# Second moving tile from the bank, rotation of the keys two steps sooner, angle steps spread over later steps

## The chip, the cores and the metric

The kernel runs on one core of a Trainium2 chip. Five engines work side by side, each through its own instructions in order: TensorE (PE, with its weight loads PEld), VectorE (DVE), ScalarE (ACT), GpSimd (POOL) and SyncE (SP), which here only issues DMAs. The metric is the device time of one execution in microseconds; the time before is a median of three runs.

## The reference

One decoder block on x of 2048 rows by 1024, in float32:

```python
ada = (c_act @ w_ada[l] + b_ada[l])[:, None, :]
shift, scale, gate = jnp.split(ada, 3, axis=-1)
h = _rms(x, g_pre[l]) * (1.0 + scale) + shift
proj = h @ w_in[l]
q, k, v, z_a, u_b, v_b, z_b, g_logits = jnp.split(proj, SPLIT_IDX, axis=-1)
q = _rope(q.reshape(b, s, N_Q_HEADS, HEAD_DIM), positions)
k = _rope(k.reshape(b, s, N_KV_HEADS, HEAD_DIM), positions)
...
y_a = _swa_with_sinks(q, k, v, sinks[l]) * jax.nn.silu(z_a)
...
merged = gate_a * (y_a @ w_proj_a[l]) + gate_b * (y_b @ w_proj_b[l])
y = merged @ w_out[l]
x = x + gate * _rms(y, g_post[l])
```

`_rms` divides each row by its root mean square; `_rope` rotates pairs of the head's columns by the cosine and sine of position times frequency. What is left out here (window attention with sinks, the spatial gating) lies behind the part of the kernel that the diff touches.

## The kernel before

**Products.** Each large matmul is done by a seven-product (Strassen-like) scheme on quarters: a product p = 0 to 6 multiplies a sum of quarters of the weights by a moving tile T[p], a sum of quarters of the activations. Each operand is split into a high part in fp32r (ScalarE copies it) and a low part (VectorE subtracts the high part from the source), and `mm3` adds high x high, high x low and low x high. So a product of a block is 12 matmuls of 128x128 by 128x512: 4 slices kt, 3 terms each.

**Steps.** The order of the work is written out by hand. `step(body)` runs the hooks registered for the step, then the body, then the hooks marked post; `later(n, f)` registers f for n steps on; a Block's `run` has hooks between its slices ("k0", "mid", "k2"). The first half of the sequence (s = 0) starts at step 0 with four weight pairs run product by product: steps 0 to 3 are product 0 of blocks 0 to 3, steps 4 to 7 product 1, and so on to product 6 in steps 24 to 27. Their banks are X/W, Y/Z, the two halves of a double bank S (shown as "s") and two banks b. In the trace, products 0, 3 and 5 of blocks 0 to 3 stand on bankX, bankY, s, b in turn, and products 1, 2, 4 and 6 on bankW, bankZ, s, b. From step 28 one pair follows the other, seven steps each (28 to 34, 35 to 41, 42 to 48), on banks X, W, Y, X, Y, Z, Y. Product 6 adds into bank Y, which VectorE must have read after product 4 (`add(c, b["Y"], self.wsb)`, line 164 in the trace).

**Weights.** `w_get` at a step prepares the weights three steps ahead: ScalarE casts the high part (line 223) and the low part is put on a list `due`. `low_now` empties that list, VectorE's subtraction standing at line 158; it is called at the next preparation.

**Moving tiles.** T[1] needs the second half's reciprocal root mean square: `rstd` sums squares on TensorE, GpSimd raises to -1/2, `rstd_out` (line 685) broadcasts the four columns over 128 partitions by four matmuls into a bank, and ScalarE copies the bank to an SBUF tile `rbs[h]` (line 690). `t_y` (line 704) multiplies each slice by that tile, `t_d` (line 762) subtracts, `t_hi` (lines 778 and 782) makes the high part on ScalarE and `t_lo` (lines 798 and 803, or 158) the low part on VectorE. `t_part` spreads the same calls for T[3] to T[6] over the steps ahead of their products.

**Rotation.** `rope_steps` is a list of 21 steps on 128x512 tiles that turn positions into angles; one of them is two ScalarE instructions (lines 625 and 626), the others are one VectorE instruction each. Eleven run in the opening, one in `second_half` ahead of `rstd_out`, nine in the post hooks of steps 9 to 17. `rope_out` takes sine and cosine on ScalarE (lines 643 and 645) and stores them. `load_rope` reads each table back in four DMAs (line 868). `rope_finish` rotates a projected tile: `turn` (lines 954 and 958) issues DMAs with swapped partitions, four steps later `mix` multiplies by sine on GpSimd and cosine on VectorE (line 962), then `both` adds and ScalarE takes the high part, then `low` subtracts. For the keys of the first half, `wait` is 15 and 9 steps after their products, which puts their turns at steps 30 and 32; those of the first queries stand at 32, 34, 36 and 37.

All DMAs named here are issued by SyncE in the same written order.

Of the kernel before, what the change touches and what calls it, by code (L numbers as in the profile page):

```python
# [50 lines left out]
NFIRST = 4  # L51
# [4 lines left out]
def hybrid_block(ctx: ExitStack, tc: tile.TileContext, xt, x, wada, wgate, wI, wP, wO,  # L56
# [30 lines left out]
    def flat(tag, dt=F32):  # L87
        return t2(tag, [P, 512], dt)
# [28 lines left out]
    kr_s = [dram(f"kr{i}", [P, TG]) for i in range(2)]  # L117
# [31 lines left out]
    BK = {b: pX.tile([P, 512], F32, tag=b, name=f"bank{b}") for b in "XYZW"}  # L149
# [79 lines left out]
    def later(n, f, post=False):  # L229
        hooks.setdefault((slot[0] + n, post), []).append(f)  # L230
# [419 lines left out]
    def rope_do(n):  # L650
        for _ in range(n):
            next(rope_it, None)
# [29 lines left out]
        rs0[h] = small(4, "rs")  # L682
        pow_rstd(rs0[h], ss, 1.0 / D)

    def rstd_out(h, b):
        for i in range(4):
            pe.matmul(b[:, i * P : (i + 1) * P], rs0[h][:, i : i + 1].broadcast_to([P, P]), ident,
                      start=True, stop=True, skip_group_check=True)
        rbs[h] = flat("e")
        act.copy(rbs[h], b)  # L690

    def positions():
# [254 lines left out]
    def rope_finish(h, R, put_out, wait, raw=None):  # L947
        st = {}

        def turn():  # L950
            nonlocal R
            if raw is not None:
                R = flat("x")
                sp.dma_start(R, raw)
            st["hi"] = flat("x", F32R)
            st["rot"] = st["hi"].bitcast(F32)
            for r in range(2):
                sp.dma_start(st["rot"][r:P:2, :], (R if raw is None else raw)[1 - r : P : 2, :])

        def mix():  # L960
            psub(st["rot"], st["rot"], ropet["s", h], ALU.mult)
            dve.tensor_tensor(out=R, in0=R, in1=ropet["c", h], op=ALU.mult)

        def both():
            add(R, R, st["rot"])
            act.copy(st["hi"], R)

        def low():
            sub(R, R, st["rot"])
        later(1 + wait, turn)  # L970
        later(5 + wait, mix)
        later(6 + wait, both, True)
        later(8 + wait, low)
        later(9 + wait, lambda: put_out(st["rot"], R))
# [8 lines left out]
    def ev_kv(s):  # L983
        def ev(key, src, psum):
            h = half(key)
            if ft(key) == 0:
                def put_out(hi, lo):
                    ks = slice(P + s * NT + h * 512, P + s * NT + (h + 1) * 512)
                    for i, t in enumerate((hi, lo)):
                        sp.dma_start(k_s[:, i, ks], t)  # L990
                R = rope_in(src, psum, "e")
                if s == 0:
                    store(1, kr_s[h], R)
                rope_finish(h, R, put_out, (15, 9)[h] if s == 0 else h, kr_s[h] if s == 0 else None)
            else:
                t = src
                if psum:
                    t = flat("e")
                    act.copy(t, src)

                def turn():
                    b = bank()
                    for c in range(4):
                        pe.transpose(b[:, c * P : (c + 1) * P], t[:, c * P : (c + 1) * P], ident)

                    def out_():
                        o = flat("qS"[s])
                        act.copy(o, b)
                        at = 1 + s * 8 + h * 4
                        store(1, v_s[:, at : at + 4, :], o.rearrange("p (a b) -> p a b", a=4))  # L1010
                    later(1, out_)
                later((3, 10)[h] if s == 0 else 2, turn, True)
        return ev
# [309 lines left out]
    def run_all():  # L1323
        nonlocal T

        for s in range(NS):
# [6 lines left out]
            if s == 0:  # L1333
                later(26, setup_sgu)
                later(28, zero_heads)
            load_rope(s, ((29, 28, 31, 30), (10, 11, 12, 13))[s])
            for i in range(8):
                later((27 + 5 * i // 2, 17 + 3 * i)[s], lambda i=i: ln_step(s, i))
            for c in range(4):
# [25 lines left out]
            if s == 0:  # L1365
# [12 lines left out]
                def second_half():  # L1378
                    ada_row(1, range(0, 1))
                    want(NFIRST)  # L1380
                    want(NFIRST + 1)
                    sum_to(NFIRST + 3)
                    low_now()
                    sum_to(NFIRST + 4)
                    rope_do(1)
                    rstd_out(1, BK["W"])
                    ada_row(1, range(1, 4))
                    t_y(1, 0)
                    for kt in range(4):
                        t_d(1, kt)  # L1390
                        t_hi(1, kt)
                        if kt < 3:
                            t_y(1, kt + 1)
                        t_lo(1, kt)
                    want(NFIRST + 3)
                    low_now()

# [18 lines left out]
                later(2 * NFIRST, fetch_all, True)  # L1416
                later(NFIRST, lambda: sp.dma_start(mcpt, mcp))
                later(NFIRST, lambda: sp.dma_start(snk8, sinks.broadcast_to([P, 8])))
                for i in range(9):
                    later(9 + i, lambda: rope_do(1), True)  # L1420
                later(26, rope_out, "mid")
                later(12, lambda: dve.tensor_scalar(out=snk8, in0=snk8, scalar1=1.0 / SM, scalar2=None, op0=ALU.mult))
                for p in range(3, 7):
                    for i, (n, post) in enumerate(((-4, True), (-3, False), (-3, True), (-2, False), (-2, True), (-1, False))):
# [218 lines left out]
```

## Time and profile before

| what | value |
|---|---|
| median of three runs | 1201.62 us (1200.4 to 1201.99) |
| the profiled execution's own time | 1203.53 us |
| its span, first to last instruction | 1201.8 us |
| TensorE busy | 1184.4 us (99%) |
| VectorE busy | 869.2 us (72%) |
| ScalarE, GpSimd busy | 644.0 us (54%), 342.4 us (28%) |
| granted TensorE clock, mean | 0.997 |

Shares of busy time are averages over the whole span. A group of matmuls is drawn with its modelled end, so groups overlap a little. In a timeline row the number in square brackets is the engine's idle time ahead of the row, and what ended it.

### The profile page before, as it was taken

How to read it: one execution, taken by the hardware profiler on the slowest of the kernel's cores; microseconds unless marked ns; L12 is line 12 of the kernel's file. 1: busy time of each engine (PE TensorE's matmuls, PEld its weight loads, DVE VectorE, ACT ScalarE, POOL GpSimd, SP SyncE). 2: the span in 40 equal slices, each digit the busy share in tenths (PEclk: the TensorE clock that was granted, in tenths of full speed). 3: DMA queues.
4: the chain of work that ended last, by engine and by line, in shares of the span. 5: the costliest groups of instructions: out<-in, count | busy, mean ns of one | idle time of the engine just before them, and what ended most of it. 6: DMA issues, size and time to landing. Idle time of an engine off the chain costs nothing.

```text
span 1201.8 us, 17373 instructions
## 1 busy us (share of the span) xinstructions
PE 1184.4 (99%) x5440; PEld 945.6 (79%) x5440; DVE 869.2 (72%) x1320; ACT 644.0 (54%) x1379; POOL 342.4 (28%) x290
## 2 busy tenths in 40 slices
PE   8999999999999999999999999999999999999997
PEld 4677878888777777888888887777778878888886
DVE  6897688678876676355866886554877977767775
ACT  5476455568765685443444766555845412444443
POOL 0001455333365201112201113130042301255453
PEclk9999999999999999999999999999999999999999
DMA  9546898959899997868779998998968987846352
GB/s 354 232 150 205 268 358 316 279 162 296 258 329 347 310 318 271 279 221 263 254 233 278 269 292 244 317 306 254 330 199 287 383 262 261 290 149 191 129 179 88
DMA packets 228548, 312.78 MB, mean 260 GB/s; under 512 B 20964, under 2 KB 103012, under 8 KB 228456
## 3 DMA queue, kind: packets, MB, share of 16 engines
q1 hardware_dynamic: 227984, 310.99, 79.5%
q8 instruction: 43, 0.70, 0.2%
q14 instruction: 49, 0.40, 0.1%
q0 software_dynamic: 176, 0.53, 0.1%
q10 hardware_dynamic: 296, 0.16, 0.1%
HBM read 201.82 MB, written 105.06 MB: 255 GB/s over the span
## 4 chain that ended last, share of the span: by engine, by line
PE 83%; DVE 6%; DMA 5%; ACT 2%; issue 2%; SPq 1%; POOL 0%; ACTq 0%; DVEq 0%; POOLq 0%
PE bankY L175 27%; PE bankX L175 19%; PE bankW L175 11%; PE bankZ L175 11%; PE b L175 3%; PE s L175 2%; PE b L1168 2%; PE s L1118 1%; PE s L1119 1%; DMA raw<-in_wP 1%; PE b L1057 1%; DVE W L158 1%; PE b L1153 1%; DMA raw<-sS 1%; DVE e L164 1%
## 5 line engine op out<-in xcount | busy, mean ns | idle before, releaser
L175 PE MATMUL bankY<-T,W 128*128 128x512 f32 x1566 | 383.2, 393 | 2.6 <-DVE e L164 2.3
L175 PEld LDWEIGHTS bankY<-T,W 128*128 128x128 f32 x1566 | 291.7, 188 | 64.3 <-issue 3.7
L158 DVE TENSOR_TENSOR W<-raw,W 128x512 fp32r<-128x512 f32 x327 | 268.5, 827 | 73.4 <-ACT W L223 70.5
L223 ACT CAST W<-raw 128x512 fp32r<-128x512 f32 x327 | 201.8, 618 | 131.0 <-PE b L175 41.9
L175 PE MATMUL bankX<-T,W 128*128 128x512 f32 x1098 | 266.9, 391 | 0.1
L175 PEld LDWEIGHTS bankX<-T,W 128*128 128x128 f32 x1098 | 204.2, 188 | 41.9 <-DVE T L803 0.5
L175 PE MATMUL bankW<-T,W 128*128 128x512 f32 x672 | 165.7, 393 | 2.9 <-DVE T L158 2.0
L175 PE MATMUL bankZ<-T,W 128*128 128x512 f32 x672 | 163.8, 391 | 0.0
L175 PEld LDWEIGHTS bankW<-T,W 128*128 128x128 f32 x672 | 124.4, 188 | 32.7 <-DVE T L158 3.5
L175 PEld LDWEIGHTS bankZ<-T,W 128*128 128x128 f32 x672 | 124.9, 188 | 27.2 <-ACT T L392 1.6
L161 POOL TENSOR_TENSOR S<-x,x 128x512 f32<-128x512 f32 x28 | 37.1, 1329 | 239.1 <-DMA x<-yb 107.8
L161 POOL TENSOR_TENSOR raw<-raw,raw 128x512 f32<-128x512 f32 x46 | 73.9, 1606 | 93.1 <-DVE W L158 44.3
L161 POOL TENSOR_TENSOR S<-raw,raw 128x512 f32<-128x512 f32 x23 | 34.9, 1518 | 168.8 <-DMA raw<-in_wI 74.5
L158 DVE TENSOR_TENSOR T<-x,T 128x512 fp32r<-128x512 f32 (+1 forms) x105 | 73.6, 748 | 3.6 <-ACT T L392 3.6
L164 DVE TENSOR_TENSOR e<-bankY,e 128x512 f32<-128x512 f32 x43 | 29.7, 690 | 59.2 <-PE bankY L175 59.0
L175 PE MATMUL b<-T,W 128*128 128x512 f32 x282 | 69.7, 390 | 0.5 <-DVE W L158 0.5
L175 PEld LDWEIGHTS b<-T,W 128*128 128x128 f32 x282 | 52.8, 188 | 11.8 <-DVE W L158 0.9
L175 PE MATMUL s<-T,W 128*128 128x512 f32 x246 | 60.1, 389 | 0.2 <-DVE e L164 0.2
L392 ACT CAST T<-x 128x512 fp32r<-128x512 f32 x100 | 56.0, 619 | 3.8 <-PE s L175 2.1
L175 PEld LDWEIGHTS s<-T,W 128*128 128x128 f32 x246 | 46.1, 188 | 10.2 <-issue 0.6
L161 POOL TENSOR_TENSOR raw<-S,raw 128x512 f32<-128x512 f32 x23 | 32.7, 1424 | 70.1 <-DVE W L158 58.5
L1147 ACT ACTIVATE P<-P,rc 128x128 f32<-128x128 f32 x128 | 44.5, 396 | 11.6 <-DVE rc L1143 11.6
(292 smaller groups left out, 1459.0 us busy)
## 6 DMA issues: line engine op xcount, KB each, us to landing
raw<-in_wI SPq DMA_DIRECT2D x127, 256.0 KB, 4.6
raw<-sS SPq DMA_DIRECT2D x92, 256.0 KB, 5.0
g<-e SPq DMA_DIRECT2D x64, 256.0 KB, 4.1
sS<-raw SPq DMA_DIRECT2D x43, 256.0 KB, 4.4
T<-in_wada SPq DMA_DIRECT2D x16, 512.0 KB, 8.2
q<-q SPq DMA_DIRECT2D x64, 128.0 KB, 5.4
q<-k_s SPq DMA_DIRECT2D x64, 128.0 KB, 4.9
raw<-m SPq DMA_DIRECT2D x32, 256.0 KB, 4.1
```

The lines of the kernel that those rows point to most:

```text
L158: dve.tensor_tensor(out=o, in0=a, in1=b, op=ALU.subtract)
L161: pool.tensor_tensor(out=o, in0=a, in1=b, op=op)
L164: dve.tensor_tensor(out=o, in0=a, in1=b, op=ALU.add)
L175: pe.matmul(o, w[:, i, sl], t[:, j, kt, :], start=start and kt == kts[0] and n == 0, stop=stop and kt == last and n == 2, skip_group_check ...
L223: act.copy(w[:, 0, :], src)
L392: act.copy(T[p][:, 0, kt, :], rs[kt])
L1057: pe.matmul(b[:, ch * P : (ch + 1) * P], st["v", h][:, ch, :], wT[:, c, :], start=True, stop=True)
L1118: pe.matmul(o, q[:, g, :], k[:, 0, :], start=True, stop=False)
L1119: pe.matmul(o, q[:, g, :], k[:, 1, :], start=False, stop=True)
L1147: act.activation(out=st["P", kv][:, g, 0:P], in_=st["P", kv][:, g, 0:P], func=AF.Copy, scale=st["rc", kv][:, g : g + 1])
L1153: pe.transpose(t[:, g * P : (g + 1) * P], st["P", kv][:, g, 0:P], ident)
L1168: pe.matmul(o[own, :], v[:, k, own], st["pv", kv][k], start=k == 1, stop=k == 0)
```

## The change

`rstd_out` takes a flag: without it the broadcast stays in its bank, `t_y` reads the bank, and `rstd_keep` copies it to SBUF later. The second half's broadcast goes to the second half of the double bank S, which block 2 first uses in step 6, in place of bank W. The angle step in `second_half` goes; ten angle steps stand in the post hooks of steps 13 to 22. `rope_out` stands at step 24 (26 before), the loads of the tables at 26 to 29 (28 to 31 before), the keys' rotation two steps sooner. `low_now` is also called at the start of step 9.

```diff
-    def rstd_out(h, b):
+    def rstd_out(h, b, kept=True):
...
-        rbs[h] = flat("e")
+        rbs[h] = b
+        if kept:
+            rstd_keep(h)
+
+    def rstd_keep(h):
+        b, rbs[h] = rbs[h], flat("e")
         act.copy(rbs[h], b)
...
-                rope_finish(h, R, put_out, (15, 9)[h] if s == 0 else h, kr_s[h] if s == 0 else None)
+                rope_finish(h, R, put_out, (13, 7)[h] if s == 0 else h, kr_s[h] if s == 0 else None)
...
-            load_rope(s, ((29, 28, 31, 30), (10, 11, 12, 13))[s])
+            load_rope(s, ((27, 26, 29, 28), (10, 11, 12, 13))[s])
...
                     sum_to(NFIRST + 4)
-                    rope_do(1)
-                    rstd_out(1, BK["W"])
+                    rstd_out(1, S[:, 1, :], False)
                     ada_row(1, range(1, 4))
                     t_y(1, 0)
...
                         t_lo(1, kt)
+                    rstd_keep(1)
                     want(NFIRST + 3)
...
-                for i in range(9):
-                    later(9 + i, lambda: rope_do(1), True)
-                later(26, rope_out, "mid")
+                later(2 * NFIRST + 1, low_now)
+                for i in range(10):
+                    later(13 + i, lambda: rope_do(1), True)
+                later(24, rope_out, "mid")
```

## Rows read from the trace of the kernel before

**Rows 1.** Page: the span, and TensorE's busy time, share of the span, instructions.

```profile
span 1201.8 us, 17373 instructions
PE 1184.4 (99%) x5440; PEld 945.6 (79%) x5440; DVE 869.2 (72%) x1320; ACT 644.0 (54%) x1379; POOL 342.4 (28%) x290
```

**Rows 2.** Windows: length, busy time of each engine, granted clock, DMA share, GB/s.

```profile
61.00:109.00 48.00, 46.16 (x197) 35.95 (x195) 46.80 (x73) 32.64 (x54) 3.48 (x2) 1.00 0.52 175
109.00:130.00 21.00, 20.79 (x95) 17.21 (x96) 7.69 (x11) 14.07 (x23) 6.56 (x6) 1.00 0.71 224
130.00:145.00 15.00, 15.00 (x69) 12.07 (x69) 10.88 (x19) 7.12 (x14) 5.68 (x7) 1.00 0.82 273
145.00:160.00 15.00, 12.66 (x60) 10.21 (x59) 14.85 (x18) 6.33 (x13) 11.23 (x11) 1.00 0.98 322
...
161.00:163.00 2.00, 2.00 (x7) 1.51 (x6) 2.00 (x4) 0.19 (x1) 1.37 (x2) 0.50 1.06 341
```

**Rows 3.** Timeline of TensorE, 42 to 164 us: start, duration, group, idle before.

```profile
42.70 0.50 PE L175 MATMUL bankW<-T,W 128*128 128x512 f32 x1 [0.21 <-ACT T L778]
43.43 0.73 PE L175 MATMUL bankW<-T,W 128*128 128x512 f32 x2 [0.22 <-DVE T L798]
...
69.12 2.57 PE L175 MATMUL b<-T,W 128*128 128x512 f32 x10 [0.46 <-DVE W L158]
...
85.28 0.73 PE L175 MATMUL bankW<-T,W 128*128 128x512 f32 x2 [0.46 <-DVE T L803]
...
105.29 1.87 PE L175 MATMUL bankW<-T,W 128*128 128x512 f32 x7
108.00 0.98 PE L175 MATMUL bankW<-T,W 128*128 128x512 f32 x3 [0.84 <-DVE T L158]
109.21 0.73 PE L175 MATMUL bankW<-T,W 128*128 128x512 f32 x2 [0.23 <-DVE T L158]
...
136.97 2.98 PE L175 MATMUL bankY<-T,W 128*128 128x512 f32 x12
...
154.35 2.88 PE L175 MATMUL bankZ<-T,W 128*128 128x512 f32 x12
159.56 4.44 PE L175 MATMUL bankY<-T,W 128*128 128x512 f32 x12 [2.34 <-DVE e L164]
```

**Rows 4.** Timeline of ScalarE: the copy of the second broadcast.

```profile
39.83 0.58 ACT L690 COPY e<-bankW 128x512 f32<-128x512 f32 x1 [1.40 <-PE bankW L687]
```

**Rows 5.** Timeline of VectorE, 40 to 159 us.

```profile
40.45 0.75 DVE L704 SCALAR_TENSOR_TENSOR q<-q,AS,e 128x512 f32<-128x512 f32 x1
...
108.47 0.68 DVE L158 TENSOR_TENSOR T<-x,T 128x512 fp32r<-128x512 f32 x1
...
138.02 1.79 DVE L962 TENSOR_TENSOR x<-x,m 128x512 f32<-128x512 f32 x1
...
145.08 1.17 DVE L962 TENSOR_TENSOR x<-x,m 128x512 f32<-128x512 f32 x1 [0.52 <-DMA x<-x]
...
150.41 1.29 DVE L164 TENSOR_TENSOR x<-x,x 128x512 f32<-128x512 f32 x2
...
155.64 2.38 DVE L158 TENSOR_TENSOR x<-x,x 128x512 f32<-128x512 f32 x2
...
158.76 0.66 DVE L164 TENSOR_TENSOR e<-bankY,e 128x512 f32<-128x512 f32 x1
```

**Rows 6.** Timeline of SyncE's queue: issue time of the DMAs, count.

```profile
115.79 0.93 SPq L646 DMA_DIRECT2D cs<-m  x2
...
133.24 0.43 SPq L954 DMA_DIRECT2D x<-kr  x1
...
141.79 1.18 SPq L958 DMA_DIRECT2D x<-x  x2
```

**Rows 7.** Groups by line and shape, VectorE: count, busy us, mean ns, idle before.

```profile
L1062 DVE SCALAR_TENSOR_TENSOR x<-b,col,Tt 128x512 f32<-128x512 f32 x16 | 11.9, 744 | 5.0 <-PE b L1057 3.4 <-issue 1.6
...
L593 DVE SCALAR_TENSOR_TENSOR T<-T 128x512 f32<-128x512 f32 x8 | 5.5, 689 | 0.5 <-ACT T L626 0.4
```

## The prediction, made before the changed kernel ran

> **What bounds the kernel now.** Read the page first: TensorE is busy 1184.4 of 1201.8 us [rows 1]. No edit here removes a matmul, so what can be won is TensorE's idle time and the time it runs at a lower clock, about 17 us over the whole span. Next, TensorE's timeline up to step 42 [rows 3] shows where it waits behind the edits: 0.21 and 0.22 us at step 4 (second tile's first slice), 0.46 at step 11 (a weight's low part), 0.46 at step 16 (a tile's low part), 0.84 and 0.23 at step 24 (low parts of the last tile), and 2.34 at step 41, for VectorE's read of bank Y. [...]
>
> Then the windows, for who makes TensorE wait. From 61 to 109 us VectorE is busy 46.80 of 48.00: it is the real bound there, with 73 instructions at 46.80/73 = 0.64 us each. From 109 to 130 it is busy 7.69 of 21, from 130 to 145 10.88 of 15, and from 145 to 160 14.85 of 15 [rows 2]. The kernel thus has two jams on VectorE with a hole between them. The edits move work inside the first jam, and from the second one toward the hole.
>
> **The second tile's products.** The chain today is broadcast, ScalarE's copy at 39.83 (0.58), VectorE's first product at 40.45 [rows 4, 5]. The copy leaves it, so the first product can start at about 39.85, 0.60 sooner. The angle step that stood ahead of it ran under the copy; taking it away here wins nothing, and it has to be done later. What does a product cost when it reads the bank? No row shows this one. The nearest is L1062, the same operation with a bank as first source: 744 ns, against 0.75 us for today's product from SBUF [rows 5, 7]. I take no surcharge; the bounds are -0.06 (L593, the same operation without a pointer operand, takes 689 ns) and +0.06 for each of four products, too little to move the range.
>
> [...]
>
> With the chain 0.60 sooner, step 4's two waits vanish: 0.43 us. The late copy costs ScalarE 0.58 behind the fourth high part, which itself is 0.60 sooner, so the casts behind it keep their time. Without that cover they would be 0.58 late, on weights used two and three steps later. Bank S's second half is needed again in step 6; steps 4 and 5 cover the copy.
>
> **The low part sooner.** The extra call puts step 11's low part ahead of two tile products on VectorE, and an angle step no longer stands in front. The wait of 0.46 at step 11 goes. Behind it the two products are 0.64 later each, which the angle step's absence pays back.
>
> **Angle steps later.** No VectorE instruction leaves the stretch from step 8 to step 24: eight were in it and, with the one from the opening of step 4, nine are in it now. Three leave steps 9 to 11 (3 x 0.64 = 1.9 us), so step 16's tile is in time and its 0.46 goes; but three more come into steps 18 to 22, just ahead of the last tile. TensorE reaches step 24 by 0.43 + 0.46 + 0.46 = 1.35 us sooner. When does the last tile's low part, at 108.47 [rows 5], end? Bounds: if the queue keeps the whole lead it has won, -0.60 (earlier start) + 0.64 (added instruction) = 0. If it loses the 1.9 us because what it reaches sooner isn't there (ScalarE's high parts, weights by DMA, and the two ScalarE angle instructions now standing in front of the fifth tile), +1.9. Nothing excludes either end; I take the middle, +1.0. So all the early gain is given back at step 24 and 1.0 more: the wait there grows from 1.07 to 1.07 + 1.35 + 1.0 = 3.4 us, in pieces between slices. This is the step I trust least.
>
> **Sine and tables.** Sine and cosine move two steps up, in front of ScalarE's reads of the results of blocks 0 and 1; their banks are next written in step 29 and later, so this hides, and if it did not, weights cast three steps ahead would come late by the time of the two instructions. The DMAs behind them: 2 stores, 16 loads of tables, 3 DMAs for each key turn. SyncE issued the stores at 115.79, the first key turn at 133.24 and the first query turn at 141.79 [rows 6]. The issues from 115.79 to 141.79 keep their number; the tables and key turns only move ahead of the others. I take the query turn as unmoved (bounds: 2 us sooner, 2 later).
>
> **Keys' rotation sooner.** Between the wait for the query's DMA (row at 145.08) and the read of bank Y (158.76) VectorE works through 13.7 us [rows 5]. Of the pair of adds at 150.41 (1.29) one leaves, of the pair of subtractions at 155.64 (2.38) one, as the first key's takes no place there any more: 0.65 + 1.19 = 1.84. So the read of bank Y can start at 158.76 - 1.84 = 156.9 and end at 157.6. GpSimd's product moves with VectorE's, past sums of weights in GpSimd's queue, which then wait behind it for the same DMA. The moved products each cost 0.7 to 1.79 (row at 138.02, with GpSimd's product running beside it) in a stretch where VectorE has 4.1 us free of 15 [rows 2, 5]. [...]
>
> TensorE would come to step 41 at 159.56 - 2.34 = 157.22 in today's time, and 1.0 later by the above, 158.2. The read of bank Y is then done: no wait, and no fall of the clock. Bounds of that read's end: 157.6, and 161 if the key products, now two steps sooner in VectorE's order, find their DMAs late and hold it for 3.4 us.
>
> **Sum.** Today step 41 starts at 159.56 and loses 1.56 to the clock: 161.1. After: 158.2. Difference -2.9 us. Behind step 41 TensorE runs without a gap, and the difference is carried to the end. The profiled execution's own time, 1203.53 (its span of 1201.8 and 1.7 around it), would become 1200.6; it lies 1.9 above the median of the runs, so the median goes from 1201.62 to 1198.7.
>
> **Rivals.**
> 1. The clock falls at step 24 too. For: 3.4 us of waits there, more than the 2.34 that went before the fall at 161. Against: they lie in pieces, and 1.07 in two pieces left it at 1.00 [rows 2, 3]. It costs 1.56 more, and step 41 is still clear: 1198.7 + 1.6 = 1200.3.
> 2. SyncE is the limit: key turns are issued hardly sooner, VectorE stands in order before products whose data isn't there, and bank Y is read as late as today or later. For: the query product already waits 0.52 for a DMA, and the turn's issue runs into 141.79. Against: the hole before 130. Step 41 then starts at 159.6 to 161 and the clock falls: 161.1 to 162.6, 0 to 1.5 above today, 1201.6 to 1203.1.
> 3. The other side: a new wait at step 34. The first key's product now stands on VectorE ahead of the read that frees bank Y for step 34, with weights' low parts behind it too. TensorE comes to step 34 at 136.97 today [rows 3], 138.0 after. The product and the read take 0.7 + 0.66 at least, so from 136.6 on each microsecond by which the key's data lands later is a microsecond of wait, and past some 2.3 the clock falls as it did at 161. Data landing at 141 gives a wait of 4.4 + 1.56; step 41 then starts at 158.2 + 6.0 = 164.2, 3.1 later than today's 161.1: 1204.7. Slower by more than a run can tell it is from a landing at about 140.3. Against: today the turn issued at 133.24 feeds a product that runs at 138.02 without a wait [rows 5, 6], and the turn now is issued sooner.
> 4. VectorE keeps its lead in the first jam: the last tile is not later, TensorE loses nothing at step 24, and VectorE has less queued behind it. -3.9 and up to 1.35 more: 1197.7 to 1196.4, 1197.0 in the middle.
> 5. That the bank's reading wins nothing on its own is already in the sum: its 0.43 is given back at step 24.
>
> **Chances.** Forecast 0.50, own range 1197.3 to 1200.1; rival 1 0.14, rival 2 0.13, rival 3 0.10, rival 4 0.13. A measurement of this kernel tells 0.2%, 2.4 us, from no change. Faster by more: 0.37 of the forecast's 0.50 and rival 4, 0.50. Within: 0.13 of the forecast, rival 1 and 0.09 of rival 2, 0.36. Slower: rival 3 and 0.04 of rival 2, 0.14. The range from 1196.8 to 1203.0 leaves out rival 3, and a part of rivals 2 and 4.
>
> **What would show it.** Right: no wait at steps 4 and 11; a wait at step 24 of 2 to 4.5 us in pieces, on VectorE's low parts; no wait of over 0.5 us at step 41 and the clock at 1.00 from 157 to 165. Products at L704 of 0.75 us with the bank as source. Wrong: the clock at 0.50 near step 24 (rival 1) or near 160 (rival 2), a wait on bank Y at step 34 (rival 3), or step 24 ending sooner than today's 109.9 (rival 4).

## The result, and the profile after

The change makes the kernel slower: 1206.75 us median (1205.4 to 1208.03, 5 runs) against 1201.62 before (1200.4 to 1203.21); ratio 1.004, 95% interval 1.0027 to 1.0053. The prediction was 1198.7. The profiled execution took 1206.75 us, 3.2 more than the profiled one of before.

The page of the changed kernel: the span, and TensorE's busy time, as in [rows 1].

```profile
span 1205.0 us, 17376 instructions
PE 1184.9 (98%) x5440; PEld 946.7 (79%) x5440; DVE 862.1 (72%) x1320; ACT 645.4 (54%) x1380; POOL 348.4 (29%) x290
```

TensorE's work is what it was; the 3.2 us are idle time and clock. The windows (columns as in [rows 2]) say in which stretch. The last two rows look closer at the clock behind the waits of step 24 and of step 41.

```profile
61.00:109.00 48.00, 45.13 (x193) 35.32 (x191) 45.86 (x72) 31.48 (x53) 3.60 (x2) 1.00 0.50 175
109.00:130.00 21.00, 20.45 (x86) 16.42 (x86) 8.48 (x12) 13.99 (x23) 3.63 (x4) 0.92 0.55 172
130.00:145.00 15.00, 14.32 (x66) 11.29 (x65) 7.41 (x14) 4.34 (x9) 5.89 (x6) 1.00 0.87 279
145.00:160.00 15.00, 15.00 (x72) 12.34 (x71) 13.36 (x18) 9.16 (x20) 9.92 (x9) 1.00 0.93 314
...
110.50:112.50 2.00, 1.99 (x5) 1.61 (x6) 1.40 (x3) 1.40 (x3) 0.00 (x0) 0.54 0.00 0
...
166.00:168.00 2.00, 2.00 (x6) 1.52 (x6) 2.00 (x4) 0.00 (x0) 1.45 (x1) 0.50 1.00 332
```

Two things stand out beside [rows 2]. The clock is now low twice, at 111 (0.54) and at 166 us (0.50), where before, in this stretch, it was low only at 161 (0.50). And VectorE did 7.41 us of work from 130 to 145 us in place of 10.88, and 13.36 in place of 14.85 up to 160: 5.0 us less by 160, though it had the same work.

TensorE's timeline from step 20 to step 42, which answers to [rows 3].

```profile
95.94 0.73 PE L175 MATMUL bankX<-T,W 128*128 128x512 f32 x2 [0.89 <-DVE T L808]
...
104.70 0.61 PE L175 MATMUL bankW<-T,W 128*128 128x512 f32 x2
105.69 0.73 PE L175 MATMUL bankW<-T,W 128*128 128x512 f32 x2 [0.38 <-DVE W L158]
106.90 0.98 PE L175 MATMUL bankW<-T,W 128*128 128x512 f32 x3 [0.47 <-DVE T L158]
109.30 0.96 PE L175 MATMUL bankW<-T,W 128*128 128x512 f32 x3 [1.43 <-DVE T L158]
110.51 1.10 PE L175 MATMUL bankW<-T,W 128*128 128x512 f32 x2 [0.24 <-DVE T L158]
111.40 4.17 PE L175 MATMUL bankZ<-T,W 128*128 128x512 f32 x12
...
140.34 0.63 PE L934 MATMUL b<-cst,q 128*128 128x128 f32 x4 [0.68 <-DMA q<-vb]
140.73 3.00 PE L175 MATMUL bankY<-T,W 128*128 128x512 f32 x12
...
164.31 4.57 PE L175 MATMUL bankY<-T,W 128*128 128x512 f32 x12 [3.31 <-DVE e L164]
```

Before, the twelve products behind step 24 were these:

```profile
109.78 2.89 PE L175 MATMUL bankZ<-T,W 128*128 128x512 f32 x12
```

The waits of steps 4, 11 and 16 are gone, as forecast; one of 0.89 us at step 20 is new. In step 24, reached 0.59 us sooner than before (104.70 against 105.29), TensorE waits 2.52 us in four pieces, and the next twelve products take 4.17 us in place of 2.89. Step 34 starts 3.8 us later than before (140.73 against 136.97), step 41 4.75 later (164.31 against 159.56), and the wait there has grown from 2.34 to 3.31 with its clock fall. TensorE itself came to step 41 at 164.31 - 3.31 = 161.00, 3.8 later than before (157.22); 0.3 of this, as of every later time here, is the opening's (the twelve products on bank S start at 31.16, before at 30.85).

Who holds step 41? Next come VectorE's rows of the changed kernel (to be held against [rows 5]), with the first product from the bank, the two products of the keys, and the read of bank Y.

```profile
40.14 0.75 DVE L709 SCALAR_TENSOR_TENSOR q<-q,AS,s 128x512 f32<-128x512 f32 x1
...
109.77 0.68 DVE L158 TENSOR_TENSOR T<-x,T 128x512 fp32r<-128x512 f32 x1
...
134.42 1.10 DVE L967 TENSOR_TENSOR x<-x,m 128x512 f32<-128x512 f32 x1 [2.40 <-DMA x<-kr]
...
145.62 0.69 DVE L967 TENSOR_TENSOR x<-x,m 128x512 f32<-128x512 f32 x1 [4.02 <-DMA x<-kr]
...
163.51 0.66 DVE L164 TENSOR_TENSOR e<-bankY,e 128x512 f32<-128x512 f32 x1
```

VectorE stands 2.40 and 4.02 us at the keys' products, whose turned data isn't there; before, both started without a wait (138.02 and 143.87). Last, SyncE's issues, which answer to [rows 6]; L873 are the loads of the tables.

```profile
114.19 0.93 SPq L646 DMA_DIRECT2D cs<-m  x2
116.72 0.32 SPq L916 DMA_DIRECT2D vb<-e  x1
...
118.09 2.44 SPq L873 DMA_DIRECT2D m<-cs  x4
120.63 0.53 SPq L916 DMA_DIRECT2D vb<-e  x1
...
122.63 2.36 SPq L873 DMA_DIRECT2D m<-cs  x4
125.09 0.58 SPq L928 DMA_DIRECT2D q<-vb  x1
...
131.68 0.58 SPq L959 DMA_DIRECT2D x<-kr  x1
...
139.36 0.43 SPq L959 DMA_DIRECT2D x<-kr  x1
...
144.86 1.14 SPq L963 DMA_DIRECT2D x<-x  x2
```

Two rows of before, the second store of block 0's result and the second key turn:

```profile
113.34 0.33 SPq L911 DMA_DIRECT2D vb<-e  x1
...
139.90 0.64 SPq L954 DMA_DIRECT2D x<-kr  x1
```

The first key turn is issued at 131.68 (before 133.24) and the second at 139.36 (before 139.90): both moved two steps up in the program, two times twelve products or some 5.8 us, but only 1.6 and 0.5 us in time. Four table loads take SyncE 2.4 us, and all 16 of them 9.7. Eight of the 16 now stand ahead of the LayerNorm's first load (125.09; before at 117.72, with none ahead of it); ahead of the two key turns stand 12 and 16, as before. The query's turn comes 3.1 us later than before (144.86 against 141.79).

### The profile page after: what moved, and what is told of

It reads as the page before. It is cut to its first block, busy times and chain, and to the rows that moved or that the text cites. A ratio compares the mean times of both kernels' runs of the same rounds, so it can differ in the third digit from the quotient of the medians.

```text
span 1205.0 us, 17376 instructions
## 1 busy us (share of the span) xinstructions
PE 1184.9 (98%) x5440; PEld 946.7 (79%) x5440; DVE 862.1 (72%) x1320; ACT 645.4 (54%) x1380; POOL 348.4 (29%) x290
## 4 chain that ended last, share of the span: by engine, by line
PE 86%; DVE 5%; DMA 2%; ACT 2%; issue 2%; SPq 1%; POOL 1%; ACTq 0%; DVEq 0%; POOLq 0%
PE bankY L175 28%; PE bankX L175 19%; PE bankW L175 12%; PE bankZ L175 11%; PE b L175 4%; PE s L175 3%; PE b L1173 2%; PE s L1123 1%; PE s L1124 1%; PE b L1062 1%; DVE W L158 1%; PE b L1158 1%; PE b L720 1%; DMA x<-kr 1%; SPq L873 1%
## 5 line engine op out<-in xcount | busy, mean ns | idle before, releaser
L158 DVE TENSOR_TENSOR W<-raw,W 128x512 fp32r<-128x512 f32 x327 | 266.2, 820 | 74.5 <-ACT W L223 72.4
L158 DVE TENSOR_TENSOR T<-x,T 128x512 fp32r<-128x512 f32 (+1 forms) x105 | 70.0, 716 | 2.8 <-ACT T L392 2.5
```

The source lines that it names most:

```text
L158: dve.tensor_tensor(out=o, in0=a, in1=b, op=ALU.subtract)
```

## The experiments

The theory after the comparison: two parts of the change cost, each in its own place. The angle steps put the last tile late, and TensorE's waits there lower its clock (**angles**). The sooner tables, sine and key turns jam SyncE's row, so that VectorE waits at the keys' products (**keys**). Rivals: the bank read itself costs; the sooner sine alone does it, through ScalarE; the transfers, not their issue, are late. Each time is the median of 5 to 12 executions; ratios are to the kernel before on the same chip and come from the single executions, so they need not equal the ratio of two medians. Times of single traces count from the span's start, and the opening varies: the twelve products on bank S start between 30.64 and 32.20 us, so a difference under some 1.5 us between two traces can be the opening's.

**The change in three parts.** The first keeps only the bank read and the sooner low part; the second adds the sooner tables, sine and turns; the third adds the later angle steps in their place; the fourth is the keys' part on the kernel before.

```
- later(24, rope_out, "mid"); tables (27, 26, 29, 28); turns (13, 7)
+ later(26, rope_out, "mid"); tables (29, 28, 31, 30); turns (15, 9)      (first, third)
- for i in range(10): later(13 + i, lambda: rope_do(1), True)
+ rope_do(1) in second_half; for i in range(9): later(9 + i, ...)         (first, second)
```

> The change without its angle steps, tables and keys: only the bank read and the low part sooner; one angle step stays in the opening of step 4 and nine at steps 9 to 17, keys and tables as before. Theory A (two separate causes: the angle steps put just ahead of the last tile make step 24 late and drop the clock there; the keys' rotation two steps sooner makes VectorE wait for DMAs that SyncE issues no sooner, and step 41 late): no clock fall at step 24, which ends 0.4 to 0.8 us sooner than before; step 41 still waits about 2.5 to 3 us and the clock falls there; time 1200.5 to 1201.6. Theory B (the bank read itself, or the extra low part, upsets the order): 1203 or more, with a clock fall at step 24.

Measured: 1202.39 us, ratio 0.9998 (0.9987 to 1.0008), above theory A's range, as were the three that follow. The clock stays up at step 24 (step 25 takes 2.90 us), but TensorE still waits 0.84 and 0.24 us there and reaches it only some 0.1 us sooner, counted from the products on bank S (105.29 - 30.85 before, 106.52 - 32.20 here). Step 41 waits as before:

```profile
160.79 4.47 PE L175 MATMUL bankY<-T,W 128*128 128x512 f32 x12 [2.34 <-DVE e L164]
```

> The change with its angle steps put back (one in the opening of step 4, nine at steps 9 to 17); keys, tables, bank read and low part as changed. Theory A: clock 1.00 at steps 24 and 25; step 41 waits for bank Y by 3 us or more with a clock fall, as VectorE stands before the keys' products until their DMAs land; time 1202 to 1204. Theory C (the angle steps alone cost the 5 us, the keys' move is a gain that they hide): no wait at step 41, 1198 to 1200.

Measured: 1204.6 us, 1.0018 (1.001 to 1.0027). Step 25 takes 2.92 us, so the clock stays up at step 24; the transposes ahead of step 34 wait 2.33 us for the LayerNorm's load, and VectorE waits 7.2 us in all at the keys' products. TensorE's transposes, step 34 and step 41:

```profile
139.23 0.63 PE L934 MATMUL b<-cst,q 128*128 128x128 f32 x4 [2.33 <-DMA q<-vb]
139.61 4.58 PE L175 MATMUL bankY<-T,W 128*128 128x512 f32 x12
...
161.81 2.97 PE L175 MATMUL bankY<-T,W 128*128 128x512 f32 x12 [0.31 <-DVE e L164]
```

So theory A had the place wrong: here the clock falls at step 34 (0.89 from 130 to 145 us), behind the wait for the LayerNorm's load, and step 41 waits only 0.31 us at full clock. VectorE's read of bank Y is late, from 161.00 (before 158.76), but TensorE comes late as well.

> The change with keys, tables and sine and cosine put back to their old steps; bank read, low part and late angle steps as changed. Theory A: step 24 waits 2.5 us in pieces and the clock falls, so that step 28 starts 2.5 to 3 us later than before; but VectorE's read of bank Y keeps its old time, so that step 41 waits little and its clock fall goes: 1200 to 1201.6 in all. Theory D (the keys' move alone costs the 5 us, the angle steps are harmless): step 24 as before, 1201 to 1202, and the clock falls at step 41.

Measured: 1203.8 us, 1.0011 (1.0 to 1.0021). Step 24 waits 0.38, 0.47 and 1.44 us, and step 25 takes 3.74; step 41 has no wait at all.

```profile
111.51 3.74 PE L175 MATMUL bankZ<-T,W 128*128 128x512 f32 x12
```

With no wait and no fall at step 41, step 42 starts at 162.72, sooner than before (164.33), and the profiled execution is no longer than the one of before (1203.01 against 1203.53). So its trace doesn't show where this version's median loses.

> The kernel before with the keys' rotation, the tables' loads and sine and cosine two steps sooner, nothing else. Theory A: SyncE issues the first query's turn no sooner than 141 us, VectorE waits 4 to 8 us in all before the two keys' products, step 41 waits 2.3 us or more and the clock falls: 1201.5 to 1203.5. Theory D: 1205 to 1207. Theory C: 1198 to 1199.

Measured: 1204.77 us, 1.0018 (1.0009 to 1.0027), with the same waits as the second: 2.23 us ahead of step 34, whose products take 4.33, and 0.25 at step 41. So the early part is worth nothing that lasts, the bank read is harmless, the keys' part loses 1.8 thousandths (2.2 us) in both runs, and with the angles the loss is 1.1 (1.3 us; the interval touches none). Added, these are 2.9 thousandths of the change's 4.0. Together the two parts also meet: with the late angles the stores of sine and of block 0 come later (second store at 120.63; 119.45 in the second version), the second key turn with them (139.36; 138.33), and the read of bank Y starts at 163.51 in place of 161.00.

**Is it the clock at step 24?** The third version, with added products of ones into the free bank X between the slices of step 24 (unused work).

```
+ for m, at in ((2, "k0"), (4, "mid"), (1, "k2")):
+     later(24, lambda m=m: warm(1, m), at)
```

> The run with bank read, low part and late angle steps (keys and tables as before) and in it three dummy matmuls of 256, 512 and 128 columns on the free bank X between the slices of step 24, where TensorE waits for VectorE's low parts: they add about 1.6 us of work inside 2.7 us of waits, and their result is not used. If the clock fell because TensorE stood idle there: granted clock 1.00 at step 25, its twelve products 2.9 us in place of 3.7, about 1 us sooner in all. If not: the clock falls all the same and the time is the same or up to 1 us longer.

Measured: 1202.76 us, 1.0003 (0.9995 to 1.0012). TensorE's timeline of that kernel from the last added group on, and step 41:

```profile
109.86 0.38 PE L551 MATMUL bankX<-ones 128*128 128x128 f32 x2
110.00 1.23 PE L175 MATMUL bankW<-T,W 128*128 128x512 f32 x3
111.07 2.89 PE L175 MATMUL bankZ<-T,W 128*128 128x512 f32 x12
...
160.31 3.01 PE L175 MATMUL bankY<-T,W 128*128 128x512 f32 x12 [1.79 <-DVE e L164]
```

Step 25 takes 2.89 us with TensorE kept busy (clock 1.00 from 109 to 130 us), and 3.74 without (0.92): the idle pieces had lowered the clock. The medians lie 1.0 us apart; the intervals overlap, so what this is worth in time is not settled. And TensorE, sooner here, now waits 1.79 us at step 41 where the third version waited none: VectorE's read sets that step.

**Which of the keys' edits?** Tables and sine alone, turns alone, and the second version with its table loads issued by GpSimd.

```
- sp.dma_start(t[at : at + 64 : 2, :] ...
+ (pool if s == 0 else sp).dma_start(t[at : at + 64 : 2, :] ...           (third)
```

> The kernel before with only sine and cosine and the sixteen table loads two steps sooner; key turns stay at steps 30 and 32. Theory E (the sixteen loads, about 0.6 us each in SyncE's order, are what push the layer norm's second load back, so that TensorE's transposes after step 33 wait): that wait is 1.5 us or more, as with the keys moved too, and the time is 1.5 to 2.5 us above before. Theory F (the key turns are the cause, since VectorE then stands before their products): no wait at the transposes, time as before.

Measured: 1205.99 us, 1.0032 (1.002 to 1.0044): more than the keys together in the ratio, though the intervals overlap. The turns are issued at 136.98 and 141.10, later than before; the transposes wait 0.91 us, less than theory E wants, and the clock fall is at step 41, which waits 4.03 us and takes 5.46.

> The kernel before with only the key turns two steps sooner, tables as before. Theory E: the second layer norm load is issued within 1.5 us of its time before, the transposes do not wait, VectorE waits 3 us or more for the keys' DMAs, step 41 within 1 us of before: same time as before within 0.15%. Theory F: a wait of 2 us at the transposes or at step 34 with a clock fall, 1.5 to 2.5 us slower.

Measured: 1203.87 us, 1.0012 (1.0003 to 1.0021). The turns are issued early (124.62 and 134.78), but VectorE waits 2.75 and 3.66 us at the same products, now for the tables, and step 41 waits 3.46 us. As theory E says, the transposes don't wait here.

> The run with bank read, low part and keys sooner and the angle steps put back, and in it the sixteen table loads of the first half issued by GpSimd's queue in place of SyncE's. Theory A/E (SyncE's issue order is the limit): the first key turn is issued at about 122 us in place of 130.6, no wait of over 0.5 us at the transposes nor at step 41, no clock fall from 120 to 170: 4 to 6 us below the run with SyncE's loads, 1198 to 1200. Rival (the transfers themselves or VectorE's load are the limit, whoever issues): the waits stay, 1203 to 1205.

Measured: 1203.33 us, 1.0006 (0.9996 to 1.0017). A miss: SyncE, with no table loads, stands 6.4 us before the LayerNorm's first load until block 0's result has landed, whose stores come late (115.55 and 116.93) because the sine stands ahead of the gelu reads; and the keys' landing takes 5.2 to 5.4 us in place of 3.1 to 3.3 in the kernel before. VectorE still waits 4.2 us for a key.

**The sine's place.** Alone, on the kernel before; then behind the gelu reads, in the second version.

```
- later(26, rope_out, "mid")
+ later(24, rope_out, "mid")          (alone, on the kernel before)
- later(24, rope_out, "mid")
+ later(25, rope_out, True)           (in the second version)
```

> The kernel before with one edit: the sine and cosine and their stores two steps sooner (step 24 in place of 26); table loads, key turns, early part and angle steps as before. In the change they stand ahead of the two gelu reads on ScalarE, and behind both in the kernel before. Theory C (the two table swaps and the two activations, some 4 us on ScalarE, delay the gelu reads and with them the stores of block 0's result and the loads of the LayerNorm): the result's first store moves from 111.4 to about 115.5 us here too, the LayerNorm's first load from 117.7 to 119 or later, and the time is 0.5 to 1.5 us over the kernel before. Theory D (the sine's place costs nothing alone, since SyncE had 4 us between store and load in the kernel before; the cost comes only with the tables and turns in SyncE's row): the LayerNorm's first load stays within 1 us of 117.7 and the ratio within 0.001 of 1.

Measured: 1207.38 us, 1.0053 (1.0037 to 1.0069): the largest ratio of any single edit here, and several times what was expected. SyncE's issues in it:

```profile
113.58 0.93 SPq L646 DMA_DIRECT2D cs<-m  x2
116.10 0.32 SPq L911 DMA_DIRECT2D vb<-e  x1
...
117.47 0.38 SPq L911 DMA_DIRECT2D vb<-e  x1
...
123.81 0.62 SPq L923 DMA_DIRECT2D q<-vb  x1
```

The second store of block 0's result goes at 117.47, 4.1 us later than before (113.34; 0.6 of it is the opening's), the LayerNorm's load waits 5.4 us for it to land, and all that stands behind that load in SyncE's row is some 5 us late: key turns at 138.90 and 145.42. Step 41 waits 3.87 us.

> The change without its angle steps, with the sine and cosine put behind the two gelu reads (one and a half steps later than in the change, half a step sooner than before); tables and key turns sooner as in the change. Theory C (sine ahead of gelu delays the stores and so the LayerNorm's load): the stores go back to 111.4 and about 113.3 us, the LayerNorm's first load is sooner than 123.8, the wait of 2.33 us ahead of step 34 shrinks to under 1, and the time is 1 us or more below the 1204.6 of the same kernel with the sine ahead. If SyncE's row of table loads alone sets that load, the wait stays at 2 us or more and the time at 1204 to 1205.

Measured: 1205.51 us, 1.003 (1.0017 to 1.0042). A miss: the first store goes back to 111.58, but the second is issued at 120.30, since sine stores and table loads now stand ahead of it in SyncE's row. The LayerNorm's load (123.87) and the wait ahead of step 34 (2.45) are where they were, and the clock falls at step 34 (4.59), not at step 41. The chain can be held up on ScalarE or on SyncE.

**What sets step 41 in the kernel before?** Its table loads by GpSimd at their old steps; and two added products of ones ahead of step 41 (unused work), with the early part and on the kernel before.

```
+ later(41, lambda: warm(2, 4))
```

> The kernel before with the 16 table loads of the first half issued by GpSimd in place of SyncE, all at their old steps. If SyncE's row of issues sets when the key turns start, and these set VectorE's arrival at bank Y for step 41, the key turns are issued some 5 us sooner than 133.2 and 139.9, the wait at step 41 goes (2.34 to under 0.5) with its clock fall, and the time falls by 2 to 4 us, to about 1199. If the turns have another limit (their turn in the program by steps, or transfers that then run together and land later), the turns move by under 2 us or land as late as before, and the ratio is within 0.001 of 1.

Measured: 1201.79 us, 0.9997 (0.9984 to 1.001). The turns go to 127.14 and 134.11, 6 us sooner, and step 41 still waits 2.02 us: from 146 us on VectorE has no wait, it is busy 14.93 of 15. So at step 41 SyncE is not the bound of the kernel before; VectorE's load is. The twelve products of step 41 take 2.99 us here, the clock at 1.00 from 160 to 175 us, and still the median shows no gain: the expected one missed. A likely reason, read from the mean clocks and shown by no second trace of the kernel before: the fall at step 41 doesn't come in every execution. Of 137 executions of the kernel before, run beside these versions, 47 had a mean granted clock of 0.999 (median 1201.1 us) and 41 one of 0.997 (1203.2 us); the profiled one, with the fall, is of the second kind. A median mixes both, and a trace shows one.

> The early part alone (bank read and low part sooner) with two added products of ones into the free bank X ahead of step 41, unused work of some 1.8 us that runs inside the 2.34 us wait there. If the wait at step 41 lowers the granted clock of the twelve products behind it (4.47 us in place of 2.9), the wait shrinks to about 0.6, the twelve take 2.9 to 3.0, and the kernel gains about 1.5 us: 1200.7 beside a kernel before of 1202.2, ratio 0.9987. If the lower clock has another reason, the twelve still take 4.4 and the ratio stays at 1.000.

> The kernel before with nothing but the two added products of ones ahead of step 41 (unused work). If the gain of the same two products on the early part (ratio 0.9984) is all the clock's at step 41, it is here too: 0.9980 to 0.9992, and the early part adds nothing that lasts. If the early part's microsecond lasts once step 41 no longer waits long, this stands at 0.9992 to 1.0000.

Measured: 1200.47 us, 0.9984 (0.9974 to 0.9995), and 1201.48 us, 0.999 (0.998 to 0.9999). Step 41 in the first (the two added products are drawn as four instructions):

```profile
156.82 1.88 PE L551 MATMUL bankX<-ones 128*128 128x512 f32 x4
159.22 3.01 PE L175 MATMUL bankY<-T,W 128*128 128x512 f32 x12 [0.52 <-DVE e L164]
```

The twelve products take 3.01 in place of 4.47: the clock's 1.5 us is won by keeping TensorE busy, in a step that starts no sooner behind step 24 (54.2 us in this run, 54.3 in the first version). In the second, step 41 has no wait and takes 3.33 us. All executions of both have a mean granted clock of 0.998 or 0.999. Whether the early part adds to it, the overlapping intervals leave open.

**The causes taken out.** The sine at its old place, tables one step sooner, turns two: with SyncE's table loads on the kernel before, then the whole change so; then both with the loads issued by GpSimd, the change with step 24 filled too; last the change without its angle steps. The diff is against the change; against the kernel before the sine is unmoved.

```
- tables (27, 26, 29, 28); later(24, rope_out, "mid")
+ tables (28, 27, 30, 29); later(26, rope_out, "mid")
```

> The kernel before with the key turns two steps sooner, as in the change, and their table loads one step sooner, the sine left at its old place behind the result's stores. Theory C (the loss of the sooner keys comes from the sine's place, by the later stores and the LayerNorm's load behind their landing): the LayerNorm's first load is issued by 121 us where the same keys with the sooner sine had 123.8, no wait over 1 us stands ahead of step 34, and the time is at least 1.2 us under the 1204.8 of that kernel: ratio 1.0008 or less. Rival S (the table loads and the turns in SyncE's row, and the key products waiting at the head of VectorE's row, cost it by themselves): ratio 1.0012 to 1.003 again.

> The whole change with one part put back: the sine at its old place, and the tables one step sooner in place of two. The lower clock at step 24 stays (1.4 us by the run that filled it). Theory C: the rest of the change's 5 us is the sine's place, so this stands 1 to 2 us over the kernel before, ratio 1.0005 to 1.0018. Rival S: ratio 1.003 or more, as in the change.

Measured: 1205.11 us, 1.0022 (1.0009 to 1.0036), and 1207.31 us, 1.0039 (1.0025 to 1.0054). Rival S holds against theory C in both: with the sine kept the loss is the same. Part of theory C did come: in the first the LayerNorm's load is issued at 121.94 and the transposes ahead of step 34 wait only 0.21 us. But the wait has moved on to step 41, with the clock fall:

```profile
161.58 5.46 PE L175 MATMUL bankY<-T,W 128*128 128x512 f32 x12 [3.07 <-DVE e L164]
```

VectorE's read of bank Y starts at 160.78 there, and in the keys' part with the sooner sine at 161.54, which is no difference when counted from the opening (129.8 us behind the products on bank S in both). TensorE, let through at step 34, now waits for that read. VectorE's rows of the first:

```profile
131.75 0.90 DVE L962 TENSOR_TENSOR x<-x,m 128x512 f32<-128x512 f32 x1 [2.48 <-DMA x<-kr]
...
142.74 0.69 DVE L962 TENSOR_TENSOR x<-x,m 128x512 f32<-128x512 f32 x1 [3.91 <-DMA x<-kr]
```

> The kernel before with the key turns two steps sooner, the tables one step sooner and the sine kept, and now the 16 table loads issued by GpSimd. If the keys' own loss is that the products went two steps up VectorE's row while SyncE, behind the table loads, issued their turns little sooner (138.84 in place of 139.90 for the second), the turns are issued by 127 and 133 us here, VectorE's two waits for the turned keys (2.48 and 3.91 us with SyncE's table loads) shrink to under 1 each, the wait at step 41 to under 2, and the ratio to 0.997 to 1.000. If the products wait for another reason (transfers that land later because more of them run together), VectorE still waits over 2 us for a key and the ratio stays at 1.001 or more.

Measured: 1201.36 us, 0.9988 (0.9977 to 0.9999), 3.4 thousandths (4.1 us) under the same schedule with SyncE's loads, each against the kernel before on its own chip. SyncE's issues of the two key turns, then VectorE's two products of the keys:

```profile
124.77 0.46 SPq L954 DMA_DIRECT2D x<-kr  x1
...
130.58 0.43 SPq L954 DMA_DIRECT2D x<-kr  x1
```

```profile
130.47 2.72 DVE L962 TENSOR_TENSOR x<-x,m 128x512 f32<-128x512 f32 x1
...
140.59 0.68 DVE L962 TENSOR_TENSOR x<-x,m 128x512 f32<-128x512 f32 x1
```

No wait at either key, though a key turn now takes about 6 us to land: it is issued soon enough. The read of bank Y starts at 158.11, 2.7 us sooner than with SyncE's loads though its opening ran 0.7 later, and step 41 waits 0.92 us, at full clock (its products take 3.01).

> The whole change with the three causes found taken out: the sine at its old place with the tables one step sooner, the table loads issued by GpSimd, and three groups of added products of ones (unused work) in the waits of step 24. If the three are all that made it slower than before, no clock fall is seen at step 24, VectorE's waits for keys are under 1 us each, and the ratio is 0.997 to 1.000. If something else of the change costs, it stays at 1.001 or more.

Measured: 1201.46 us, 0.9987 (0.9978 to 0.9997). With these three edits, the sine at its old place with the tables one step and the turns two steps sooner, the loads on GpSimd and step 24 filled, the rest of the change costs nothing that shows: step 25 takes 2.89 us, step 41 waits 1.03 and takes 2.99. The fill was not left out by itself in this version, so its share is not known.

> The change without its angle steps (so no wait to fill at step 24), the sine at its old place, the tables one step sooner and issued by GpSimd. As a version that could beat both: 0.996 to 0.999 if the early microsecond lasts and the keys' products no longer wait; 1.000 to 1.002 if VectorE's load ahead of step 41 sets that step anyway.

Measured: 1200.21 us, 0.9985 (0.9973 to 0.9998). It beats both kernels, the one before by 0.15%, which is under the 0.2% that a measurement here tells; the early part with step 41 filled does as much, and the intervals don't tell these versions apart.

## Why the prediction was wrong, point by point

**Right.** The waits of steps 4, 11 and 16 went. The bank read had no surcharge: the four products from the bank take 743 to 748 ns, the eight later ones from SBUF 744 to 748. The bound of +0.06 us a product was the author's estimate, and no row showed it. The gain was given back at step 24, as forecast: the last low part started 1.3 us later (109.77 against 108.47; 1.0 without the opening's 0.3), forecast 1.0. That the size came out too is in part luck: the prediction counts three more angle steps in steps 18 to 22, and the trace has five there on VectorE. That the early part wins nothing by itself held (0.9998).

**The first step that failed: the sum has no clock term at step 24.** The waits there were smaller than forecast (2.52 against 3.4 us), a new wait of 0.89 at step 20 having given back a part already. But the clock fell behind them. This is rival 1, given 0.14; it was priced at 1.56, like step 41 in the sum (4.44 - 2.88, two rows of [rows 3]), and measured as 4.17 - 2.89 = 1.28 us at step 25. The argument against it, that 1.07 us in two pieces had left the clock up, did not reach to 2.5 us in four; in the third version the same pieces were followed by 3.74 us, and filled with added products by 2.89.

**The second, and the larger: "keys' rotation sooner", with "I take the query turn as unmoved".** The prediction counted what VectorE saves when a key's pieces move up its row (1.84 us), and took the keys' data to be there when the moved products come up. It wasn't: SyncE's row between the sine's stores and the query's turn has little slack: the stores went only 1.6 us sooner (114.19 against 115.79), the 16 table loads take 9.7 us of issue, 12 and 16 of them still ahead of the two key turns, and the LayerNorm's first load stands in the same row, where it waited for a store to land 0.5 us in the kernel before and 5.4 with the sine alone. So products went two steps up in VectorE's row, and their data 0.5 to 1.6 us. VectorE then stood 6.42 us with all its other work behind it. The bound of 161 us for the end of the read was too near: it ended at 164.17 (forecast 157.6). This is rival 2, given 0.13 and priced at 0 to 1.5 us; the price missed that a wait early in VectorE's row, in the hole, empties the hole (7.41 us of work from 130 to 145 in place of 10.88) and so pushes the jam behind it. As TensorE was late too, only a part of this shows as a wait: step 41 waited 3.31 us where none was forecast. The runs show it both ways: 1.0022 with SyncE's loads, 0.9988 with GpSimd's.

**The third: "Sine and tables ... so this hides".** The cover named was the banks, which are written late. What was not covered is the next reader in memory: the gelu results go to a store, the LayerNorm's load waits for its landing, and SyncE waits with it (5.4 us in the run with the sine alone). A term was put at nothing here as well: in the changed kernel sine and cosine, with a table load of 1.28 us on ScalarE ahead of them and one behind, hold ScalarE from 112.24 to the first gelu read at 116.09; before, the gelu reads went at 110.83 and 112.71. Alone the sooner sine costs 4.9 us in the medians (1.0053). Inside the change it isn't to be seen as a cost of its own: with the sine put back and the tables a step later the change is as slow (1.0039); the 16 table loads still take 9.7 us of SyncE's row, all ahead of the second key turn, issued at 141.39 there. Whether the sine alone costs more than the whole change, the intervals leave open (1.0037 to 1.0069, and 1.0027 to 1.0053). A reason why it could is read from the traces only: with the turns moved up too, the second is issued at 139.36, not 145.42.

**Rivals taken as exclusive.** Rivals 1 and 2 sit in different stretches and came together. Rival 3's place, a wait on bank Y at step 34, showed none; the 0.68 us ahead of step 34 is the transposes' wait for the LayerNorm's load, which no rival named. Without the late angles or with the sine behind the gelu reads it is 2.2 to 2.5 us, and the clock falls at step 34, whose products take 4.3 to 4.6.

Not settled: how the loss divides. The parts alone add to 2.9 of 4.0 thousandths, and their intervals allow for all of it. The parts don't simply add: a wait taken away at one step comes up at the next, and a late TensorE hides a late read of bank Y (second version: from 161.00 in place of 158.76, with a wait of 0.31 us). Of the 4.75 us that step 41 starts later the profiled span shows only 3.2. The rest comes back mostly in one step far behind the edits: at 963.55 us TensorE waits 0.90 us for a low part (L158) in the trace of before, and has no such wait in the changed kernel's. No edit touches that step, so the 3.2 us between two single traces is not the change's cost to the tenth; the ratio of the medians is.

## What to carry to other kernels

Moving a step up moves its consumer in one queue and its producer in another: before counting a gain, write down by how much each of the two moves in time (here some 5.8 us in the program became 1.6 and 0.5 us for the two turns), and look at the issuing queue's slack, counting small DMAs one by one (the 16 table loads took 9.7 us of SyncE). A wait at the head of a busy engine's row can cost not what that instruction costs but what stands behind it: here VectorE stood 6.42 us at two products of 1.10 and 0.69, and the read of bank Y far behind them started at 163.51 in place of 158.76. Taking one wait away may do no more than move the loss to the next step at which the same engine waits: with the keys sooner, putting the sine back and the tables one step later took the wait ahead of step 34 from 2.23 to 0.21 us, and that of step 41 went from 0.25 to 3.07. Look there before counting the gain. And rivals in different stretches add up: give the chance of any of them, not of each against the rest.

## What the runs showed of the hardware

Behind waits in pieces TensorE's clock fell here as behind one wait: behind 0.38, 0.47, 1.43 and 0.24 us in step 24 the next twelve products took 4.17 us (clock 0.54 from 110.5 to 112.5), behind 0.84 and 0.23 in the kernel before 2.89. Of single waits at step 41, 1.79 and 2.02 us left its twelve products at 2.99 to 3.01, and 2.34 to 4.03 gave 4.4 to 5.5; 2.23 to 2.45 us ahead of step 34 gave 4.3 to 4.6. Added products with no use, 1.9 us of them ahead of step 41, won 1.3 us in the medians on the kernel before, and 2.0 with the early part.

A load from memory that needs a store's result held SyncE's whole row: 5.4 us in the run with the sine alone, 6.4 with GpSimd's table loads.

With the table loads on GpSimd's queue the keys' turns were issued sooner and landed slower: 5.2 to 6.1 us from issue to landing in place of 3.1 to 3.3 in the kernel before, at a DMA share of 1.05 to 1.07 from 130 to 145 us (before 0.82). Where they were issued by 125.1 and 131.1 us, VectorE had no wait at the keys all the same.
